# A decoder block on one Trainium2 core: where the token sums of the second half of the tokens are made

## The chip, the cores and the metric

The kernel runs as one program on one core of a Trainium2 chip. The core has five engines that matter here: TensorE (PE in the profile, with its weight loads as PEld), VectorE (DVE), ScalarE (ACT), GpSimd (POOL) and SyncE (SP), which in this kernel only issues DMA transfers. Each engine works through its own instructions in order. ACT also issues transfers, in order with its other work. The metric is the device time of one execution in microseconds (us); lower is better.

## The reference, cut to what matters

The block works on x of 2048 tokens with 1024 channels, in float32:

```python
h = _rmsnorm(x, norm_pre_mix)
proj = h @ w_in                                  # 1024 -> 5376
# three dilated attention groups, a chunked gMLP branch, merged by two sigmoid gates
y = merged @ w_out
x = x + _rmsnorm(y, norm_post_mix)

h = _rmsnorm(x, norm_pre_mlp)
a = relu(h @ w_mlp_in)                           # 1024 -> 4096
y = (a * a) @ w_mlp_out                          # 4096 -> 1024
x = x + _rmsnorm(y, norm_post_mlp)
```

What the change touches lies between `x = x + _rmsnorm(y, norm_post_mix)` and the first product of the MLP: how the transposed h gets from the one to the other.

## The kernel before

**The parts.** Part 1 (up to about 1120 us of the span) makes the projections, the attention and the gMLP branch. Part 2 merges the branches, multiplies by w_out, adds to x, normalizes, and transposes h. It goes by chunks of 512 tokens in the order 2, 3, 0, 1 (`chunks`, line 977), and in each chunk by four blocks of 128 tokens (`out_block`, line 900). Then comes the MLP: its first stage (h times w_mlp_in, relu and square), about 1449 to 2095 us, and its second stage (times w_mlp_out) up to the end.

**Every product is made of three.** A float32 operand is split into a rounded high part and the rest (`split`, line 67: ACT copies the high part, DVE subtracts it from the raw values), and a product is hi*hi + hi*lo + lo*hi, three matmuls. So an operand is ready for TensorE only when ACT and then DVE have split it.

**The first stage** uses a scheme with seven block products in place of eight. The tokens are worked in two halves of 1024, first tokens 1024 to 2047 (`first_half` = 1, chunks 2 and 3), then 0 to 1023 (`second_half` = 0, chunks 0 and 1). The right operands of a half are B11, B21 and B22, which are quarters of the transposed h, and T1 to T4, sums and differences of such quarters: the token sums. B11 and B21 are read from `h2_d`, a DRAM tensor of the transposed h; T1 to T4 and B22 from `t_d`, a DRAM tensor of the token sums. The left operands come from w_mlp_in, 256 columns at a time, numbered q = 0 to 15: A11 and A12 are plain quarters, S1 to S4 are sums that POOL makes of the raw weights with four instructions (`add_a`, lines 1064 to 1067), and A22 is plain. Product i of q, written (q, i), takes the pair `TERMS[i]`: 1 is A11 with B11, 2 is A12 with B21, 3 is S4 with B22, 4 is A22 with T4, 5, 6 and 7 are S1 to S3 with T1 to T3. Each is twelve matmuls (line 1093). (q, 2) adds to the bank of (q, 1), whose content ACT first copies to `xs` (line 1107).

**How the token sums are made before.** The second chunk of each half (`second = c % 2`, chunks 3 and 1) has, per block: two loads of the other chunk's transposed h from `h2_d` (line 924, on SP), the block's own transposes on TensorE (line 945) and two copies of them by ACT (line 946), four subtractions on POOL (lines 950 to 953), and the stores of five results to `t_d` (line 959; one transfer in chunk 3, three in chunk 1, where the tile is made of three places, tags `yt0` to `yt5`, line 1184). The first chunk of each half (2 and 0) stores its copies to `h2_d` instead (line 948). A block's second part (transposes, copies, sums) is put off and called by `flush`, its stores by `store`.

**The seam.** When chunk 1's last matmuls are issued, two blocks still wait to be flushed, and TensorE goes on with products of the first stage. From there to product (0, 3) the order on all engines is the order of the code (`as_written`, lines 1238 to 1297); low parts are held back until the product before them has been issued (`behind_product`, `rest`). SP's transfers in this stretch are: T2, raw weights for (3,1) and (2,2), the weights of q = 0, T3, raw weights for (4,1) and (3,2) in one tile, the stores of the flushed blocks, T1, the weights of q = 1, the raw weights for (4,2), the last block's stores, T4, B22, the weights of q = 2. A raw weight loaded alone goes to tag `ar`, which has two places, and is called by its q and n (n = 0 for A11, 1 for A12), so the raw weights for product (4, 2) are `raw_lone(h, 4, 1)`. From product (0, 3) on the order on ACT, DVE, POOL and SP is again that of a planner, which sends each engine the first instruction in code order that its own costs say is ready; TensorE's order is always that of the code.

**The rest of the first stage.** `order` lists the products; the loop at line 1334 asks for weights 14 products ahead and for their sums and splits 6 ahead. `ends` holds the last use of each right operand in the first half; behind it, `load_b` or `load_t` loads that of the second half into the same place.

Of the kernel before, what the change touches and what calls it, by code (L numbers as in the profile page):

```python
# [8 lines left out]
F32 = mybir.dt.float32  # L9
F32R = mybir.dt.float32r  # L10
# [31 lines left out]
def block_kernel(ctx, tc, a, out):  # L42
# [857 lines left out]
    def out_block(c, i, mg, mid):  # L900

        t0 = c * 512 + i * P
        isl = slice(i * P, (i + 1) * P)
        xt = bot.tile([P, D], F32, name=f"xr_{c}{i}", tag="xr")
        sp.dma_start(xt, x[t0:t0 + P, :])
        ss = sm.tile([P, 2], F32, name=f"ss_{c}{i}", tag="ss2")
        pp = [psum_mm(f"o_{c}{i}{n}") for n in range(2)]

        ks = [(n, k) for n in range(2) for k in range(KT)]
        if i == 0:  # L910
            ks.remove((0, KT - 1))
            ks.insert(KT + 2, (0, KT - 1))
        for m, (n, k) in enumerate(ks):
            if m == KT:
                mid()
            nsl = slice(n * 512, (n + 1) * 512)
            m = mg[k // 4]
            mm3(pp[n], m[:, 0, k % 4, isl], m[:, 1, k % 4, isl], wo[k][:, 0, nsl], wo[k][:, 1, nsl], k == 0, k == KT - 1)
        second = c % 2

        tt = tt_tile(c, i)
        if second:
            for o in range(2):
                sp.dma_start(tt[3 * o], h2_d[:, o * 4:o * 4 + 4, t0 - 512:t0 - 512 + P])
        y1 = bot.tile([P, D], F32, name=f"y1_{c}{i}", tag="y1", bufs=2)
        for n, p in enumerate(pp):
            nsl = slice(n * 512, (n + 1) * 512)
            junk = psum_aux(f"junk_{c}{i}{n}")
            act.activation(junk, p, AF.Square, accum_out=ss[:, n:n + 1])
            dve.tensor_mul(y1[:, nsl], p, gpost[:, nsl])  # L930
        s1 = sm.tile([P, 1], F32, name=f"s1_{c}{i}", tag="s1")
        dve.tensor_add(s1, ss[:, 0:1], ss[:, 1:2])
        r = rstd_of(sm, s1, 1, 1.0 / D, f"post{c}{i}")
        dve.scalar_tensor_tensor(xt, y1, r, xt, op0=OP.mult, op1=OP.add)
        s2 = sm.tile([P, 1], F32, name=f"s2_{c}{i}", tag="s2")
        act.activation(y1, xt, AF.Square, accum_out=s2)
        act.dma_start(x1_d[t0:t0 + P, :], xt)
        r2 = rstd_of(sm, s2, 1, 1.0 / D, f"pm{c}{i}")
        dve.scalar_tensor_tensor(y1, xt, r2, gmlp, op0=OP.mult, op1=OP.mult)
        yield  # L940
        for k in range(0, KT, 4):
            pt = psum_aux(f"pt_{c}{i}{k}")
            ht = tt[4 if k else 2] if second else tt[k // 4]
            for kk in range(4):
                pe.transpose(pt[:, kk * P:(kk + 1) * P], y1[:, (k + kk) * P:(k + kk + 1) * P], ident)
            act.activation(ht, pt.rearrange("p (k t) -> p k t", k=4), AF.Copy)
            if not second:
                act.dma_start(h2_d[:, k:k + 4, t0:t0 + P], ht)
        if second:
            pool.tensor_sub(tt[0], tt[2], tt[0])  # L950
            pool.tensor_sub(tt[1], tt[4], tt[0])
            pool.tensor_sub(tt[2], tt[4], tt[2])
            pool.tensor_sub(tt[3], tt[3], tt[1])
        yield
        if second:
            eng = act if store_eng is None else store_eng
            dst = t_d[c // 2].rearrange("p o k t -> p (o k) t")[:, :, i * P:(i + 1) * P]
            for o, t in tt["whole"]:
                eng.dma_start(dst[:, o * 4:o * 4 + t.shape[1]], t)
        yield  # L960
# [31 lines left out]

    def load_b(half, name):

        w = r3.tile([P, 2, 4, 512], F32R, name=f"{name}_{half}", tag=name, bufs=1)
        for k in range(0, 4, 2):
            t0, k0 = half * HALF, k + (4 if name == "B21" else 0)
            split_in(w[:, :, k:k + 2], h2_d[:, k0:k0 + 2, t0:t0 + 512], None, "act")
        b_[half, name] = w

# [25 lines left out]
    def raw_lones(half, *which):  # L1026

        w = wp3.tile([P, 2, 4, P], F32, name=f"w1r_lone{half}{which[0][0]}", tag="w1r", bufs=5)
        for m, (q, n) in enumerate(which):
            raw_lone(half, q, n, w[:, m])  # L1030
# [150 lines left out]
    def tt_tile(c, i):  # L1181

        if c == 1:
            w = [bot.tile([P, D], F32, name=f"tt{c}{i}{n}", tag=f"yt{i % 2 * 3 + n}").rearrange("p (k t) -> p k t", t=P)
                 for n in range(3)]
            whole = [(0, w[0]), (2, w[1]), (4, w[2][:, :4])]
            parts = {o: w[o // 2][:, o % 2 * 4:o % 2 * 4 + 4] for o in range(5)}
        else:
            w = ttp.tile([P, 5, 4, P], F32, name=f"tt{c}{i}", tag="tt")
            whole = [(0, w.rearrange("p o k t -> p (o k) t"))]  # L1190
            parts = {o: w[:, o] for o in range(5)}
        parts["whole"] = whole
        return parts
# [5 lines left out]
    for n, c in enumerate(chunks):  # L1199
        if n:  # L1200
            mg = merge(c, yt, {0: flush, 2: flush, 3: store, 6: store})
        for i in range(4):
            store()
            b = out_block(c, i, mg, flush_older)
            next(b)
            last.append(b)
            if n < 3 and not i:
                yt = load_y(chunks[n + 1])
                for dt in range(2):
                    for wch in range(2):  # L1210
                        load_gate(chunks[n + 1], dt, wch)
            if n == 3 and i == 1:
                e2r.close()
                rx = stack(e3, "rx", 1, side="right")
                r3 = stack(er, "r3", 1, side="right")
                for name in ("B11", "B21"):
                    load_b(1, name)
                for o, (q, n_) in enumerate(FIRST):
                    raw = gtp.tile([P, 512], F32, name=f"ar{n_}_{q}", tag=f"gt{o % 2}", bufs=3 - o % 2)
                    lone_a(1, q, n_, raw.rearrange("p (k c) -> p k c", k=4))  # L1220
# [17 lines left out]
    with as_written():  # L1238
        behind_product, store_eng = [], sp
        raw_t(h, "T2", tt_["T2"])  # L1240
        raw_lone(h, 3, 0)
        raw_lone(h, 2, 1)
        load_a(h, 0)
        raw_t(h, "T3", tt_["T3"])
        raw_lones(h, (4, 0), (3, 1))
        begin(0, 1)
        begin(1, 1)

        flush()
        store()  # L1250
        raw_t(h, "T1", tt_["T1"])
        split_t(h, "T2", (0,))
        begin(0, 2)
        load_a(h, 1)
        add_a(h, 0)
        split_t(h, "T2", (2,))
        split_lone(h, 3, 0)
        begin(2, 1)
        split_lone(h, 2, 1)
        begin(1, 2)  # L1260
        split_lone(h, 4, 0)
        begin(3, 1)
        raw_lone(h, 4, 1)

        flush()
        split_a(h, 0, "S2")
        split_lone(h, 3, 1)
        split_a(h, 0, "S1")
        begin(2, 2)
        store()  # L1270
        raw_t(h, "T4", tt_["T4"])
        raw_t(h, "B22", tt_["B22"])
        split_t(h, "T3")
        split_lone(h, 4, 1)
        begin(4, 1)
        split_a(h, 0, "S3")
        add_a(h, 1)
        begin(0, 6)
        split_t(h, "T1")
        begin(3, 2)  # L1280
        split_a(h, 0, "A22")
        begin(4, 2)
        split_a(h, 0, "S4")
        split_a(h, 1, "S2")
        split_t(h, "T4", (0,))
        begin(0, 7)
        split_t(h, "T4", (2,))
        split_a(h, 1, "S1")
        load_a(h, 2)
        begin(0, 5)  # L1290
        split_a(h, 1, "S3")
        split_t(h, "B22", (0,))
        begin(1, 6)
        split_t(h, "B22", (2,))
        begin(0, 4)
        behind_product, store_eng = None, None
        begin(0, 3)
# [31 lines left out]
    def raw_need(half, q, i):  # L1329
        if (half, q) not in araw and not (i < 3 and alone(q)):  # L1330
            load_a(half, q)

    n_last = order.index((second_half, NQ - TRAIL, 6))
    for n, z in enumerate(order[:n_last]):
        for z2 in order[n:n + 14]:
            raw_need(*z2)
        for z2 in order[n:n + 6]:
            if z2[:2] != (second_half, NQ - 2) or z2[2] < 3:
                need(*z2)
            elif z2[:2] not in sums_:  # L1340
                add_a(*z2[:2])
        product(*z)
        for name, last_use in ends.items():
            if z == last_use:
                (load_b if name in ("B11", "B21") else load_t)(second_half, name)
    er.close()
    middle.close()

# [426 lines left out]
```

## Time and profile before

| | us |
|---|---|
| median of three runs | 2731.72 (2729.7 to 2736.3) |
| the profiled execution's own time | 2733.0 |
| span of its profile, first to last instruction | 2731.3 |

| stretch of the span | us |
|---|---|
| parts 1 and 2, up to the first product of the MLP | 0 to 1448.7 |
| the seam, up to product (0, 3) | 1448.7 to 1505.9 |
| the MLP's first stage behind it | 1505.9 to 2095 |
| the MLP's second stage | 2095 to 2731.3 |

The time of an execution is some us longer than its span. In the profile a row of the timeline gives the start, the length, the engine, the line, the operation, what is written and read (out<-in, buffer numbers left out), and in brackets how long the engine was idle before and what released it. SPq and ACTq are the queues that issue transfers; the length in such a row is that of the issue, or of several issues merged in one row, and not that of the transfer. The windows give the busy time of each engine in a stretch, the clock granted to TensorE as a share of full speed, and how busy the 16 DMA engines were.

### The profile page before, as it was taken

To read this page: it belongs to the slowest core of one execution; us is meant where nothing else is said; L and a number is where in the kernel's file an instruction comes from. 1 tells how busy PE (TensorE), PEld (TensorE's weight loads), DVE (VectorE), ACT (ScalarE), POOL (GpSimd) and SP (SyncE) were. 2 spreads that over 40 slices of the span, in tenths; PEclk is the share of its full clock that TensorE was granted. 3 is DMA by queue.
4 is the path that set the end of the run, shared out by engine and by line. 5 is a ranking of instruction groups with operands and counts; after the bars stand their busy time and mean duration, and the time that the engine had idled before them with its cause. 6 is when DMAs were issued, how large, how long until landed. Compare 5 with 4: busy or idle time off the path is not lost. (4 is left out here: it accounts for less than half of the span.)

```text
span 2731.3 us, 34716 instructions
## 1 busy us (share of the span) xinstructions
PE 2688.8 (98%) x12674; PEld 2230.0 (82%) x12674; DVE 1583.9 (58%) x2677; ACT 1054.8 (39%) x2149; POOL 929.5 (34%) x750
## 2 busy tenths in 40 slices
PE   9999999999999999999998999999999999999998
PEld 8888888888888888787787788788887888888886
DVE  5655553344444345756567644655437887888866
ACT  5213111144444422444445545555544333333334
POOL 0351352200050023102005423223314766676645
PEclk9999999999999999999999999999999999999999
DMA  7445446366677755745559434654343222222236
GB/s 269 165 146 174 153 144 214 102 200 197 184 246 203 197 173 175 234 150 176 161 172 302 131 116 121 198 157 126 105 144 107 77 63 85 86 85 86 91 104 213
DMA packets 329725, 425.47 MB, mean 156 GB/s; under 512 B 52050, under 2 KB 205906, under 8 KB 329555
## 3 DMA queue, kind: packets, MB, share of 16 engines
q1 hardware_dynamic: 238016, 370.22, 43.2%
q10 hardware_dynamic: 91538, 53.03, 6.5%
q8 instruction: 100, 1.64, 0.3%
q14 instruction: 71, 0.57, 0.1%
HBM read 282.47 MB, written 140.71 MB: 155 GB/s over the span
## 5 line engine op out<-in xcount | busy, mean ns | idle before, releaser
L1627 PE MATMUL ya<-T_spots,s 128*128 128x512 f32 x1176 | 292.4, 392 | 3.4 <-ACT T_spots L70 3.4
L1627 PEld LDWEIGHTS ya<-T_spots,s 128*128 128x128 f32 x1176 | 221.5, 188 | 52.5 <-ACT T_spots L70 3.8
L70 ACT ACTIVATE s<-sraw 128x768 fp32r<-128x768 f32 (+1 forms) x184 | 127.4, 696 | 339.0 <-POOL sraw L1424 150.8
L1093 PE MATMUL aa<-B,A 128*128 128x512 f32 x768 | 186.8, 395 | 6.0 <-ACT xs L1107 5.2
L78 DVE TENSOR_TENSOR s<-sraw,s 128x512 fp32r<-128x512 f32 x171 | 179.5, 1074 | 6.8 <-ACT s L70 6.8
L1093 PEld LDWEIGHTS aa<-B,A 128*128 128x128 f32 x768 | 145.3, 190 | 40.0 <-ACT xs L1107 5.7
L1064 POOL TENSOR_TENSOR s<-w1r 128x512 f32<-128x512 f32 x32 | 42.3, 1322 | 395.1 <-DVE S L78 326.5
L1627 PE MATMUL yc<-T_spots,s 128*128 128x512 f32 x624 | 160.8, 391 | 0.0
L72 POOL TENSOR_SCALAR w_g<-w_g_r 128x1024 fp32r<-128x1024 f32 x32 | 34.1, 1082 | 344.8 <-PE g L97 316.1
L95 PE MATMUL x<-hT_a,wq 128*128 128x512 f32 x384 | 149.7, 390 | 0.0
L97 PE MATMUL x<-hT_a,wq 128*128 128x512 f32 x384 | 149.4, 389 | 0.0
L96 PE MATMUL x<-hT_a,wq 128*128 128x512 f32 x384 | 149.4, 389 | 0.0
L709 DVE TENSOR_REDUCE o<-po 128x256 f32<-128x512 f32 x48 | 33.1, 690 | 185.5 <-PE po L708 185.5
L1627 PEld LDWEIGHTS yc<-T_spots,s 128*128 128x128 f32 x624 | 117.2, 188 | 25.7
L70 ACT ACTIVATE hl<-r 128x512 fp32r<-128x512 f32 x48 | 30.4, 633 | 238.1 <-POOL r L307 89.0
L78 POOL TENSOR_TENSOR T_spots<-w2r,T_spots 128x512 fp32r<-128x512 f32 x70 | 104.5, 1520 | 7.5 <-ACT T_spots L70 7.5
L95 PE MATMUL g<-hT_b,w_g 128*128 128x512 f32 x256 | 104.8, 409 | 0.0
L95 PE MATMUL g<-hT_a,w_g 128*128 128x512 f32 x256 | 104.3, 407 | 0.0
L95 PE MATMUL o<-wo,mg 128*128 128x512 f32 x256 | 100.7, 393 | 2.8 <-ACT mg L70 1.6
L70 ACT ACTIVATE S<-w1r 128x512 fp32r<-128x512 f32 x96 | 60.0, 629 | 110.2 <-PE ac L1093 64.8
L1423 POOL TENSOR_TENSOR sraw<-sraw 128x256 f32<-128x256 f32 x56 | 41.4, 740 | 178.3 <-DVE s L78 163.9
L97 PE MATMUL o<-wo,mg 128*128 128x512 f32 x256 | 100.0, 391 | 0.5 <-DVE mg L78 0.4
(388 smaller groups left out, 7192.2 us busy)
## 6 DMA issues: line engine op xcount, KB each, us to landing
w1r<-in_w_mlp_in_dram SPq DMA_DIRECT2D x64, 512.0 KB, 3.6
sraw<-sd SPq DMA_DIRECT2D x128, 256.0 KB, 3.5
qk<-hl SPq DMA_DIRECT2D x24, 1024.0 KB, 5.6
qq<-qk SPq DMA_DIRECT2D x96, 256.0 KB, 5.0
w_g_r<-in_w_in_dram SPq DMA_DIRECT2D x32, 512.0 KB, 5.0
gated<-gt SPq DMA_DIRECT2D x64, 256.0 KB, 3.4
sd<-u ACTq DMA_DIRECT2D x64, 256.0 KB, 3.6
w2r<-in_w_mlp_out_dram SPq DMA_DIRECT2D x16, 1024.0 KB, 7.9
```

The costliest lines, as they stand in the source:

```text
L70: act.activation(hi, src, AF.Copy)
L72: pool.tensor_scalar(hi, src, 1.0, 1.0, op0=OP.mult, op1=OP.mult)
L78: (pool if lo_eng == "pool" else dve).tensor_sub(lo, src, f32(hi))
L95: pe.matmul(ps, lh, rh, start=start, stop=False)
L96: pe.matmul(ps, lh, rl, start=False, stop=False)
L97: pe.matmul(ps, ll, rh, start=False, stop=stop)
L709: dve.tensor_reduce(ot[:, :, j * 64:(j + 1) * 64], po.rearrange("p (b h e) -> p b e h", b=4, h=2), axis=AX.X, op=OP.add)
L1064: pool.tensor_add(s1, a21, a22)
L1093: pe.matmul(p, w[:, l, k, :], h[:, r, k, :], start=i in (1, 6, 5) and not k and not n, stop=k == 3 and n == 2, skip_group_check=True)
L1423: pool.tensor_add(a22, a21, a22)
L1627: pe.matmul(p, s[:, l], w[r], start=i in (1, 2, 5) and not m and not o, stop=m == 1 and o == 2, skip_group_check=True)
```

## The change

It has four parts. First, only chunk 3 still makes token sums in its blocks. Chunk 1 stores its transposed h to `h2_d`, as chunk 0 does (on SP where `store_eng` is set). Its tiles are one place each (`yt0` to `yt3`). Second, a new function `sums_t(k)`, called four times behind products (5, 4) to (8, 4) of the first half, loads quarters of the stored h of both chunks, makes the four sums with four subtractions on POOL, and stores them to `t_d`. Third, B22 of the second half is loaded from `h2_d` by `load_b`. Fourth, at the seam, the raw weights for (4, 2) go to a place of their own (`spare`, one of the six places of tag `xs`) and are asked for early, and T4 and B22 are asked for where those weights were, ahead of the last flush.

```diff
-        second = c % 2
+        second = c == 3
...
             if not second:
-                act.dma_start(h2_d[:, k:k + 4, t0:t0 + P], ht)
+                (act if store_eng is None else store_eng).dma_start(h2_d[:, k:k + 4, t0:t0 + P], ht)
...
     def load_b(half, name):
 
-        w = r3.tile([P, 2, 4, 512], F32R, name=f"{name}_{half}", tag=name, bufs=1)
+        w = (bp if name == "B22" else r3).tile([P, 2, 4, 512], F32R, name=f"{name}_{half}", tag=name, bufs=1)
         for k in range(0, 4, 2):
-            t0, k0 = half * HALF, k + (4 if name == "B21" else 0)
+            t0, k0 = half * HALF + (512 if name == "B22" else 0), k + (0 if name == "B11" else 4)
...
         if c == 1:
-            w = [bot.tile([P, D], F32, name=f"tt{c}{i}{n}", tag=f"yt{i % 2 * 3 + n}").rearrange("p (k t) -> p k t", t=P)
-                 for n in range(3)]
-            whole = [(0, w[0]), (2, w[1]), (4, w[2][:, :4])]
-            parts = {o: w[o // 2][:, o % 2 * 4:o % 2 * 4 + 4] for o in range(5)}
+            w = bot.tile([P, D], F32, name=f"tt{c}{i}", tag=f"yt{i}").rearrange("p (k t) -> p k t", t=P)
+            whole = []
+            parts = {o: w[:, o * 4:o * 4 + 4] for o in range(2)}
...
                 rx = stack(e3, "rx", 1, side="right")
+                spare = rx.tile([P, 512], F32, name="ar1_4", tag="xs", bufs=LEAD + 1)
...
         raw_lones(h, (4, 0), (3, 1))
+        raw_lone(h, 4, 1, spare.rearrange("p (k c) -> p k c", k=4))
         begin(0, 1)
...
         begin(3, 1)
-        raw_lone(h, 4, 1)
+        raw_t(h, "T4", tt_["T4"])
+        raw_t(h, "B22", tt_["B22"])
 
         flush()
...
         store()
-        raw_t(h, "T4", tt_["T4"])
-        raw_t(h, "B22", tt_["B22"])
         split_t(h, "T3")
...
+    eq = ExitStack()
+    tq = stack(eq, "tq", 1)
+
+    def sums_t(k):
+
+        w = tq.tile([P, 2, 512], F32, name=f"tq{k}", tag="tq", bufs=1)
+        b11, b12 = w[:, 0], w[:, 1]
+        b21, b22 = (wp3.tile([P, 512], F32, name=f"tq{k}{n}", tag="ar", bufs=2) for n in range(2))
+        t0 = second_half * HALF
+        for t, kk, c in ((b11, k, 0), (b12, k, 1), (b22, k + 4, 1), (b21, k + 4, 0)):
+            sp.dma_start(t, h2_d[:, kk, t0 + c * 512:t0 + c * 512 + 512])
+        pool.tensor_sub(b11, b12, b11)
+        pool.tensor_sub(b12, b22, b12)
+        pool.tensor_sub(b22, b22, b11)
+        pool.tensor_sub(b21, b21, b22)
+        for name, t in (("T1", b11), ("T3", b12), ("T2", b22), ("T4", b21)):
+            sp.dma_start(t_d[second_half][:, T_AT.index(name), k], t)
...
         product(*z)
+        if z[0] == first_half and z[2] == 4 and z[1] in range(5, 9):
+            sums_t(z[1] - 5)
+            if z[1] == 8:
+                eq.close()
         for name, last_use in ends.items():
             if z == last_use:
-                (load_b if name in ("B11", "B21") else load_t)(second_half, name)
+                (load_b if name[0] == "B" else load_t)(second_half, name)
```

## The prediction

> **What bounds the kernel now.** I read the page first, then TensorE's waits, then its order of time where the code touched by the diff runs, and last the queues of the engines that it waits for there.
>
> ```profile
> PE 2688.8 (98%) x12674; PEld 2230.0 (82%) x12674; DVE 1583.9 (58%) x2677; ACT 1054.8 (39%) x2149; POOL 929.5 (34%) x750
> ```
>
> TensorE is the bound, and the diff adds and removes no matmul. So the change can only win or lose what TensorE spends waiting, plus what a wait does to its clock. Two of TensorE's longer waits, at chunk 3's end (L945) and at the start of the second MLP stage (L1627), lie where the diff touches nothing. Those from 1300 to 1560 us are (us in total, times, longest):
>
> ```profile
> PE aa L1093 <- ACT xs L1107: 5.2, 1, 5.2
> PE ac L1093 <- DVE B_first L85: 1.6, 2, 1.0
> PE o L95 <- ACT mg L70: 1.2, 1, 1.2
> PE aa L1093 <- DVE A L85: 0.7, 1, 0.7
> ```
>
> The third is chunk 0's. The others lie at the seam from chunk 1 into the MLP's first stage. In chunk 1 itself TensorE waits for nothing, so what goes there is worth nothing by itself. At the seam the order of time on TensorE is (start, length, instructions, wait before):
>
> ```profile
> 1454.94 8.87 PE L1093 MATMUL aa<-B,A 128*128 128x512 f32 x38
> 1464.54 2.59 PE L1093 MATMUL aa<-B,A 128*128 128x512 f32 x10 [0.72 <-DVE A L85]
> 1466.96 1.03 PE L945 MATMUL pt<-ident,y 128*128 128x128 f32 x8
> ...
> 1473.30 3.21 PE L1093 MATMUL ab<-T_first,S 128*128 128x512 f32 x12
> 1476.35 2.93 PE L1093 MATMUL aa<-B,A 128*128 128x512 f32 x12
> 1484.53 5.52 PE L1093 MATMUL aa<-B,A 128*128 128x512 f32 x12 [5.25 <-ACT xs L1107]
> 1489.88 2.94 PE L1093 MATMUL ab<-T_first,S 128*128 128x512 f32 x12
> ...
> 1501.03 0.39 PE L1093 MATMUL ac<-B_first,S 128*128 128x512 f32 x1
> ...
> 1505.94 2.96 PE L1093 MATMUL ab<-T_first,S 128*128 128x512 f32 x12
> 1508.73 2.95 PE L1093 MATMUL ac<-T_first,S 128*128 128x512 f32 x12
> ```
>
> An undisturbed group of twelve takes 1508.73 - 1505.94 = 2.79 us, so one matmul 0.232. The losses at the seam are then:
> - products (3,2) and (4,2), from 1476.35 to 1489.88: 13.53 us for two groups, 13.53 - 5.58 = **7.95 lost**. Only 5.25 of it is the wait; the twelve matmuls behind it take 5.35 instead of 2.79.
> - (0,2) to (3,1), 1454.94 to 1466.96: 12.02 us for 48 matmuls, 48 x 0.232 = 11.14, **0.88 lost**.
> - (0,6), 1473.30 to 1476.35: 3.05, **0.26 lost**.
> - (0,3), 1501.03 to 1505.94: 4.91, **2.12 lost**.
>
> Why the matmuls behind the wait are slow, and how loaded the seam is, the windows say (busy of PE, PEld, DVE, ACT, POOL, granted clock, DMA share, GB/s):
>
> ```profile
> 1484.50:1489.40 4.90, 4.80 (x10) 3.31 (x11) 4.90 (x4) 4.14 (x6) 3.95 (x3) 0.50 1.08 328
> 1448.70:1503.80 55.10, 48.02 (x204) 37.63 (x202) 41.23 (x43) 32.33 (x52) 33.66 (x22) 0.94 0.96 324
> 1503.80:1553.00 49.20, 48.63 (x210) 39.22 (x209) 32.38 (x41) 25.09 (x43) 25.09 (x17) 1.00 0.43 134
> ```
>
> After the long idle time the clock stands at 0.50 for about five us. And through the whole seam the DMA engines are full (0.96), while just behind it they are not (0.43). So a transfer asked for late arrives late. Who made ACT late, by the queues of ACT and SP:
>
> ```profile
> 1470.46 1.33 ACT L946 ACTIVATE tt<-pt 128x512 f32<-128x512 f32 x2 [2.70 <-POOL w1r L1067]
> 1483.36 0.63 ACT L70 ACTIVATE A<-ar 128x512 fp32r<-128x512 f32 x1 [5.54 <-DMA ar<-in_w_mlp_in_dram]
> ```
> ```profile
> 1457.61 0.97 SPq L1023 DMA_DIRECT2D w1r_lone<-in_w_mlp_in_dram  x2
> 1460.06 6.57 SPq L959 DMA_DIRECT2D td<-tt  x3
> ...
> 1475.46 0.68 SPq L1023 DMA_DIRECT2D ar<-in_w_mlp_in_dram  x1
> ```
>
> The raw weights for product (4,2) are asked for at 1475.46, behind the stores of token sums, and have landed when ACT goes on at 1483.36. ACT, in order, stands 5.54 us before the split of them; behind it stands the copy L1107 that empties the bank which product (4,2) adds to.
>
> **The change part by part.**
>
> *Spare place for the raw weights of (4,2).* The load moves to the slot behind the two w1r_lone loads, 1460.06 at the latest, since the old queue issues its next DMA there. Landing, from the two loads just before it:
>
> ```profile
> DMA to landing us min/median/max: 7.9/8.1/8.2
> ```
>
> 1460.06 + 8.2 = 1468.3, 15 us earlier. What is late next is ACT's own queue. TensorE, 0.88 ahead, ends (3,1) at 1466.1; then ACT does the copy of xs (0.6), two of tt (1.1, to 1468.0), three splits of 0.6 (1469.7), two steps on c after (2,2) ends (1.3) and a DMA issue (0.6; 1471.6), two splits of T3 (2.0), the split for (4,2) (0.6) and L1107 (0.6): 1474.8. TensorE gets to (4,2) at 1489.88 - 5.35 - 1.14 - 5.25 = 1478.1. Margin 3.3 us: the wait goes, and with it the slow clock, **-7.95**.
>
> *Sums out of chunk 1.* Gone from each of the four row blocks: two loads (L924), four subtractions on POOL, three stores; in their place two stores of 256 KB. ACT's 2.70 before tt goes too: that tile waited for the place that block 1's stores still held (the row names POOL, which had long ended), and now has a place of its own. POOL's sums of weights for q = 0 stand behind token sums, and POOL's work slows DVE:
>
> ```profile
> 1463.89 1.73 POOL L1064 TENSOR_TENSOR s<-w1r 128x512 f32<-128x512 f32 x1
> ```
> ```profile
> 1462.71 3.47 DVE L85 TENSOR_TENSOR A<-ar,A 128x512 fp32r<-128x512 f32 x2
> 1490.75 0.68 DVE L85 TENSOR_TENSOR A<-w1r,A 128x512 fp32r<-128x512 f32 x1
> 1500.08 2.31 DVE L85 TENSOR_TENSOR B_first<-B_first 128x1024 fp32r<-128x1024 f32 x1
> ```
>
> The same DVE subtraction (128x512) takes 0.68 alone and 1.74 beside POOL. The two at 1462.71 are the operand that (3,1) waits for: without POOL's block-2 sums the first is done by 1463.4 and **-0.88** follows; S2 of (0,6), whose sums start at 1463.89 behind the token sums, can start when its weights have landed: **-0.26**. After that DVE's margins are the thin ones: by the same walk its half of the split for (4,2) is done at 1477.0 against 1478.5, and T1's at 1482 against 1485.
>
> *(0,3) stays.* Its two waits come from DVE reaching B_first at 1500.08, and then running beside POOL's sums of weights for q = 2. Both are tied to TensorE's own progress (the bank of (0,4) is read between the two B_first halves), not to the landing of B22. **0**; bounds -2.12 (both go) and +1.
>
> *T4 and B22 ahead of the second flush.* Four loads come earlier; the last two stores of chunk 1 come later, behind them. They hold yt3, which S4 of q = 0 takes. By the queue's throughput (324 GB/s; about 10 MB ahead of them from 1449) they land at 1480 to 1482, and ACT wants the place at 1482.6. **0**; at most +4, two slow landings.
>
> *New work in the first stage (four times).* Per k: four loads of 256 KB, four POOL subtractions, four stores; the trace has no such rows. Nearest (KB, us to landing):
>
> ```profile
> tt<-h2d SPq DMA_DIRECT2D x16, 256.0 KB, 3.7
> td<-tt SPq DMA_DIRECT2D x3, 256.0 KB, 6.3
> ```
>
> Loads 3.7 to 8.2, subtractions 4 x 1.30 to 1.73 (both lengths in the POOL rows here), stores 3.7 to 6.3: 12.6 to 21.4 us each, 50 to 86 for all. The planner sends what it can at once: these two weights are loaded 167 us ahead of their split.
>
> ```profile
> 1495.78 0.81 SPq L1023 DMA_DIRECT2D ar<-in_w_mlp_in_dram  x2
> 1662.40 0.63 ACT L70 ACTIVATE A<-ar 128x512 fp32r<-128x512 f32 x1
> ```
>
> So I expect the sums to run from about 1490 on, not at their line, in POOL's gaps (25.09 busy of 49.20 above). Cover is wide there: the T operands are wanted only in the second half of the tokens, over 200 us later, and DMA stands at 0.43. SP's stores now wait for POOL, and behind them on SP stand the loads of later weights, which are asked for 14 products ahead (14 x 2.79 = 39 us), longer than a whole set takes. If it failed, the cost is that of the slower rival below. I take **0**, bounds 0 to +8, the DVE time that 16 subtractions of POOL could hold there (16 x 0.5, from 0.68 above to 1.20 in rival 4's row).
>
> [...]
>
> Loads of B22 from h2_d, the other order of places and the moved lone loads at the stage's end cost nothing: they have over 20 us.
>
> **Sum**: -7.95 - 0.88 - 0.26 = -9.1 on the profiled execution's 2733.0 (span 2731.3), so 2723.9. The median of before is 2731.7, 1.3 below that execution: 2722.6.
>
> **The rivals.**
> 1. *(0,3) clears too* (POOL's sums of q = 2 come later than B_first, because token sums stand before them): -11.2, **2720.5**. Against it: the DVE add between the halves.
> 2. *A shorter wait takes the old one's place at the seam*: the late stores that hold yt3, or the thin DVE margins. For it: DMA at 0.96. Price up to 4: -5.1, **2726.6**.
> 3. *POOL in order, slower.* Token sums that wait for their loads stand in front of POOL's sums of weights. The lead there, by the rows of q = 8 in the settled stage:
>
> ```profile
> 1599.46 1.30 POOL L1064 TENSOR_TENSOR s<-w1r 128x512 f32<-128x512 f32 x1 [13.71 <-DVE S L78]
> 1602.22 1.62 POOL L1066 TENSOR_TENSOR w1r<-s,w1r 128x512 f32<-128x512 f32 x1
> 1614.45 2.94 PE L1093 MATMUL ab<-T_first,S 128*128 128x512 f32 x12
> ```
>
> From 1603.84 to 1614.45 are 10.6 us, less two for the splits. Four subtractions (5.2 to 6.9) plus a wait for landing (3.7 to 8.2) are 8.9 to 15.1, so it decides once a set holds POOL beyond 8.6 us out of turn; it then costs up to 6.5 a set, and past a wait like (4,2)'s the half clock for 2.6 more. At 4.5, the middle of 0 and 9.1, and four sets: +18 - 9.1 = +9, **2740.6**. Against it: the 13.71 us of idle time before each set.
> 4. *DVE held by POOL in the first stage*:
>
> ```profile
> 1601.48 1.20 DVE L78 TENSOR_TENSOR S<-w1r,S 128x512 fp32r<-128x512 f32 x1
> ```
>
> If all 8 us come through, -1, **2730.6**. Against it: DVE is busy 32 of 49 us there.
> 5. *It doesn't do what it says*: the planner leaves ACT as late by another load: **2731.7**.
>
> **How the numbers follow.** A measurement of this kernel tells 0.3%, 8.2 us, from no change; the forecast lies just beyond it. Chances: forecast 0.47 (0.43 of it beyond 8.2), rival 1 0.10, rival 2 0.22, rival 3 0.10, rival 4 0.08 (0.02 of it slower), rival 5 0.03. Faster 0.43 + 0.10 = 0.53; slower 0.10 + 0.02 = 0.12; same 0.35. The range goes from just below rival 1, 2719, to 2731, which takes in rivals 2 and 4 and leaves rival 3, half of the rest and what no case foresees: two in ten.
>
> **What would show it.** In the profile after: no wait on L1107 and a granted clock of 1.00 from (4,2) on; the load for (4,2) right behind the w1r_lone loads; ACT's tt copies without a wait; the two waits on B_first still there; token sums on POOL between 1485 and 1570, and no TensorE wait from there to 1700. The prediction is wrong if TensorE waits on ACT S or DVE S in 1480 to 1570, or if (4,2) still waits over 3 us.

## The result, and the profile after

The changed kernel takes 2742.83 us (median of five executions, 2740.25 to 2743.71) against 2732.17 for the kernel before, measured beside it (five, 2729.7 to 2736.3). The ratio is 1.0034, with a 95% interval of 1.0022 to 1.0046: it is slower by about 0.3%, where 0.3% faster was forecast. The profiled execution has a span of 2741.5 us, 10.2 longer than before.

TensorE's busy time on the page, and then the waits of TensorE that answer to those shown of before (total, times, longest):

```profile
PE 2695.7 (98%) x12674; PEld 2232.7 (81%) x12674; DVE 1572.8 (57%) x2677; ACT 1056.6 (39%) x2149; POOL 922.8 (34%) x750
```
```profile
PE ab L1093 <- DVE u L1118: 7.0, 4, 3.1
...
PE ac L1093 <- ACT B_first L70: 4.2, 1, 4.2
...
PE aa L1093 <- ACT A L70: 3.0, 1, 3.0
...
PE ac L1093 <- DVE B_first L85: 1.5, 1, 1.5
```

The long wait on L1107 is gone, as forecast. Three others have come, and the order of time on TensorE says where:

```profile
1464.73 5.98 PE L1093 MATMUL aa<-B,A 128*128 128x512 f32 x12 [3.04 <-ACT A L70]
...
1502.08 0.79 PE L1093 MATMUL ac<-B_first,S 128*128 128x512 f32 x1 [4.23 <-ACT B_first L70]
1504.40 4.63 PE L1093 MATMUL ac<-B_first,S 128*128 128x512 f32 x11 [1.52 <-DVE B_first L85]
...
1536.44 5.49 PE L1093 MATMUL ab<-T_first,A 128*128 128x512 f32 x12 [3.09 <-DVE u L1118]
```

Each of the three is followed by matmuls at half clock (windows of the same kernel; the clock stands behind POOL's column):

```profile
1464.70:1470.50 5.80, 5.65 (x12) 3.86 (x13) 2.61 (x4) 2.73 (x5) 0.00 (x0) 0.50 1.04 411
1502.00:1508.80 6.80, 5.20 (x12) 3.77 (x13) 4.57 (x4) 2.24 (x4) 6.57 (x4) 0.53 0.95 297
1536.40:1542.00 5.60, 5.56 (x13) 4.41 (x14) 3.56 (x5) 1.89 (x3) 0.53 (x2) 0.50 0.58 144
```

By the starts of single matmuls against 0.232 us each, the losses are **A**, 6.1 us at product (3,1); **B**, 8.4 at (0,3); **C**, 6.1 at 1536; and 3.2 in small ones between them. Together they are 23.8, where the same stretch of before lost 11.1 (8.0, 2.1 and 1.0). That is 12.7 more; the first stage starts 1.7 earlier than in the execution of before, and the rest of the span differs by under 1: 10.2 in all.

**Where A comes from.** ACT around it:

```profile
1456.91 0.63 ACT L1103 ACTIVATE c<-c 128x512 f32<-128x512 f32 x1
1462.51 0.54 ACTq L1099 DMA_DIRECT2D sd<-c  x1
1463.10 1.06 ACT L70 ACTIVATE T_first<-T_first 128x1024 fp32r<-128x1024 f32 x1 [5.55 <-DMA w1r_lone<-in_w_mlp_in_dram]
1464.06 0.61 ACT L70 ACTIVATE A<-ar 128x512 fp32r<-128x512 f32 x1
```

c is ready at 1457.54, but ACT issues the store of it only at 1462.51, 4.97 us later, and everything behind that issue waits too, the split for (3,1) among it. What ended the idle time, says the row, is a load of w1r_lone, which has nothing to do with c. The two loads of it were issued on SP's queue at 1451.64 and 1453.09; for that tile and stretch the profile says when they landed:

```profile
L1023 SPq DMA_DIRECT2D w1r_lone<-in_w_mlp_in_dram x2: 333/333/333, 1451.6 to 1453.1; - x2
...
DMA to landing us min/median/max: 9.3/9.8/10.2
```

1453.09 + 9.3 = 1462.4, and 0.1 later ACT's store goes. The trace gives the reason. Each issue of SP and ACT in it names the signal (a semaphore) that tells its landing, and the 1194 of them use eight such signals between them, numbers 100, 102 and 105 to 110. No transfer is issued before the one that had its signal last has landed, in all 1038 cases of this trace for which the landing before is known, and in all 1020 of before's; the nearest issue begins 0.02 us behind that landing. ACT's store had drawn the signal of the second w1r_lone load (105), which landed at 1462.44.

**Where B comes from.** The same thing a second time, on ACT:

```profile
1495.10 0.63 ACT L1103 ACTIVATE u<-u 128x512 f32<-128x512 f32 x1
1499.89 0.52 ACTq L1099 DMA_DIRECT2D sd<-u  x1
1500.45 0.63 ACT L70 ACTIVATE S<-w1r 128x512 fp32r<-128x512 f32 x1 [4.72 <-DMA w1r<-in_w_mlp_in_dram]
1500.99 1.99 ACT L70 ACTIVATE B_first<-B_first 128x1024 fp32r<-128x1024 f32 x2
```

The w1r load that had the store's signal (102) was issued at 1492.63 and landed at 1499.81; the store goes at 1499.89. SP's queue shows what it stood behind (and, in its first row, that the load into the spare place went early, as the change meant), and POOL's order what comes of it:

```profile
1454.64 0.33 SPq L1023 DMA_DIRECT2D ar<-in_w_mlp_in_dram  x1
1455.90 0.33 SPq L1343 DMA_DIRECT2D tq<-h2d  x1
...
1483.82 6.50 SPq L1349 DMA_DIRECT2D td<-tq  x4
1490.43 2.15 SPq L1343 DMA_DIRECT2D tq<-h2d  x4
1492.63 0.42 SPq L1052 DMA_DIRECT2D w1r<-in_w_mlp_in_dram  x1
...
1514.91 1.90 SPq L1343 DMA_DIRECT2D tq<-h2d  x4
1520.11 0.32 SPq L1349 DMA_DIRECT2D td<-tq  x1
1520.53 1.83 SPq L1052 DMA_DIRECT2D w1r<-in_w_mlp_in_dram  x4
```
```profile
1518.78 1.30 POOL L1344 TENSOR_TENSOR tq<-tq 128x512 f32<-128x512 f32 x1 [4.33 <-DMA tq<-h2d]
...
1524.40 1.29 POOL L1064 TENSOR_TENSOR s<-w1r 128x512 f32<-128x512 f32 x1 [0.21 <-DMA w1r<-in_w_mlp_in_dram]
```

The first load of a token-sum set goes in the middle of the seam, and POOL has made all four sets by 1524.2. Their stores on SP wait for POOL, the loads of the next set wait behind them, and behind those stand the weights.

**Where C comes from.** The weights for the next columns are asked for at 1520.53 there; POOL can begin their sums at 1524.40, and ACT's split of the first of them waited 9.02 us:

```profile
1525.73 0.63 ACT L70 ACTIVATE S<-s 128x512 fp32r<-128x512 f32 x1 [9.02 <-POOL s L1064]
```

Behind that split the subtractions on DVE come late too, and DVE stands in them when TensorE needs the sum u that empties the bank for its next product. That is the wait of 3.09 us at 1536.44:

```profile
1534.04 1.75 DVE L78 TENSOR_TENSOR A<-w1r,A 128x512 fp32r<-128x512 f32 x1
1535.71 0.67 DVE L1118 TENSOR_TENSOR u<-xs,ab 128x512 f32<-128x512 f32 x1
```

In the kernel before, the issue of those weights and POOL's first sum of them come ten us earlier (SP's queue, then POOL), and TensorE loses nothing there:

```profile
1510.29 18.51 SPq L1052 DMA_DIRECT2D w1r<-in_w_mlp_in_dram  x6
```
```profile
1514.13 1.29 POOL L1064 TENSOR_TENSOR s<-w1r 128x512 f32<-128x512 f32 x1 [8.36 <-DMA w1r<-in_w_mlp_in_dram]
```

### The profile page after: what moved, and what is told of

Same layout as the page of the kernel before. It is cut to its first block, busy times and chain, and to the rows that moved or that the text cites. A ratio compares the mean times of both kernels' runs of the same rounds, so it can differ in the third digit from the quotient of the medians.

```text
span 2741.5 us, 34740 instructions
## 1 busy us (share of the span) xinstructions
PE 2695.7 (98%) x12674; PEld 2232.7 (81%) x12674; DVE 1572.8 (57%) x2677; ACT 1056.6 (39%) x2149; POOL 922.8 (34%) x750
## 5 line engine op out<-in xcount | busy, mean ns | idle before, releaser
L95 PE MATMUL g<-hT_b,w_g 128*128 128x512 f32 x256 | 104.8, 409 | 0.0
L95 PE MATMUL o<-wo,mg 128*128 128x512 f32 x256 | 100.6, 393 | 1.0 <-ACT mg L70 0.9
L97 PE MATMUL g<-hT_b,w_g 128*128 128x512 f32 x256 | 100.4, 392 | 0.0
```

The source lines that it names most:

```text
L95: pe.matmul(ps, lh, rh, start=start, stop=False)
L97: pe.matmul(ps, ll, rh, start=False, stop=stop)
```

## The experiments

Three theories were to be told apart. **S**: a store of ACT's is held until an SP load lands whose signal it has drawn, and ACT's splits stand behind it (A). **P**: the token sums run too early, and their transfers on SP and their sums on POOL stand ahead of the weights (B and C). **D**: the seam's loads are simply late, because the DMA engines are full (0.96 of them busy in before's seam), whoever issues what.

**1. The spare place alone** (with the earlier T4 and B22 that belong to it; token sums as before):

```diff
+                spare = rx.tile([P, 512], F32, name="ar1_4", tag="xs", bufs=LEAD + 1)
...
+        raw_lone(h, 4, 1, spare.rearrange("p (k c) -> p k c", k=4))
...
-        raw_lone(h, 4, 1)
+        raw_t(h, "T4", tt_["T4"])
+        raw_t(h, "B22", tt_["B22"])
...
-        raw_t(h, "T4", tt_["T4"])
-        raw_t(h, "B22", tt_["B22"])
```

> The kernel before with the spare place for the raw weights of (4,2) and the earlier T4 and B22, the token sums of chunk 1 left where they were. Theory S (landing slots: an issue waits until an earlier transfer that had its slot has landed, the slots are dealt in the planner's order over SP and ACT, so ACT's own stores of s come to wait for SP's loads): SP is as late here as before, so ACT's first store gets an early slot; the 5.25 us wait on L1107 and its slow clock go, about 8 us are won: 2722 to 2727. Theory P (only the token sums in the first stage cost time): the same, 2723. Theory D (the DMA engines are full and whatever is asked for lands late): the wait moves to another load, 2729 to 2733.

Measured: 2733.99 against 2733.11, ratio 1.0003 (0.9993 to 1.0012). The wait on L1107 ahead of (4,2) is gone here too, and a loss of 7.5 us, nearly as large as the 8.0 that went, stands at (3,1). TensorE, then ACT:

```profile
1470.54 0.73 PE L1093 MATMUL aa<-B,A 128*128 128x512 f32 x2 [3.31 <-ACT A L70]
```
```profile
1468.32 0.54 ACTq L1099 DMA_DIRECT2D sd<-c  x1
1468.91 1.06 ACT L70 ACTIVATE T_first<-T_first 128x1024 fp32r<-128x1024 f32 x1 [5.82 <-DMA w1r_lone<-in_w_mlp_in_dram]
```

The store of c, ready at 1463.08, was held 5.24. So the edit meant for the wait moves the wait, and gains nothing. Judged by the time alone, D's forecast is the nearest and those of S and P fail; S had expected an early signal for this store, and it had that of a w1r_lone load.

**2. The token sums alone**, without the spare place and the earlier T4 and B22 (the other three parts of the diff).

> The changed kernel without the spare place and with T4 and B22 asked for where they were before. Theory S: SP runs ahead without the stores of sums, ACT's stores get late slots, a wait at (3,1) or near it and the early sums' waits after the seam stay: 2738 to 2746. Theory P: the waits after the seam stay (about 16 us lost), the seam itself loses what it lost before: 2741. Theory D: less traffic in the seam, 2730 to 2735.

Measured: 2736.08 against 2733.11, ratio 1.0010 (1.0000 to 1.0019). No store of ACT's is held over 1 us, and (3,1) loses 0.9: A belongs to the spare place. There is no wait on L1107 ahead of (4,2) either, without the spare place. B (6.7) and C (5.0) stay, so they belong to the sums. The time lies between the forecasts of the three theories and meets none.

B comes another way here, since no store is held. TensorE, then DVE:

```profile
1497.57 5.06 PE L1093 MATMUL ac<-B_first,S 128*128 128x512 f32 x11 [3.86 <-DVE B_first L85]
```
```profile
1489.57 2.35 DVE L85 TENSOR_TENSOR T_first<-T_first 128x1024 fp32r<-128x1024 f32 x1
```

That subtraction takes 1.22 in the kernel before, and the split of S behind it 1.79 here against 0.69. Both run here beside POOL's token sums (1489.54 to 1494.76), and in before while POOL is idle (1488.61 to 1498.31). With the two splits of S ahead of them (2.40 here, 1.29 in before) that is 3.3 us more, and DVE gets to B_first late. So the early sums can bring B in two ways: by a held store, as in the changed kernel, or by a DVE that takes longer beside POOL, as here.

**3. The whole change, the sums held to their line**: the planner may issue nothing of a set before the last instruction that SP and POOL were given ahead of it.

```diff
-            sums_t(z[1] - 5)
+            with ExitStack() as es:
+                for e in (mybir.EngineType.SP, mybir.EngineType.Pool):
+                    es.enter_context(tc.issue_after(next(i for i in reversed(nc.cur_bb.bb.instructions) if i.engine == e)))
+                sums_t(z[1] - 5)
```

> The changed kernel with each of the four sets of token sums queued behind the last load and the last POOL instruction traced before it, so that the planner can't send them ahead to the seam. Theory S: the wait at (3,1), 6 us with the slow clock, stays, since ACT's first store still has the slot of a w1r_lone load; those at (0,3) and (1,4) go but for about 2 us: 2727 to 2731. Theory P: the seam is clean too, 2722 to 2724. Theory D: 2724 to 2728.

Measured: 2728.64 against 2733.11, ratio 0.9981 (0.9972 to 0.9990), 14.2 below the change. The sums begin at 1571, 1591, 1610 and 1629, between POOL's sums of weights (the first row of them below), at no cost that TensorE shows; B is back at the 2.1 that before has, C is gone, and 3.5 are left at (3,1), where the store of c was held 4.31. P stands for B and C; its forecast of a clean seam fails. S's forecast comes true: A is a cost of its own.

```profile
1571.56 1.56 POOL L1344 TENSOR_TENSOR tq<-tq 128x512 f32<-128x512 f32 x1 [8.26 <-DMA tq<-h2d]
```

**4. The whole change, the seam's stores of c and u issued by SP:**

```diff
-            act.dma_start(s_d[q, half][:, :, o, :], t.rearrange("p (i c) -> p i c", i=4))
+            (act if store_eng is None else store_eng).dma_start(s_d[q, half][:, :, o, :], t.rearrange("p (i c) -> p i c", i=4))
```

> The changed kernel with the stores of s in the seam issued by SP in place of ACT; the sums stay early. Theory S: ACT waits for no slot in the seam, so the wait at (3,1) goes and that at (0,3) shrinks to about 2 us; the one at (1,4), where POOL's sums of weights come late, stays: 2730 to 2736. Theory P: all waits stay, 2741 to 2744. Theory D: they stay too, under other names, 2740 or more.

Measured: 2739.34, ratio 1.0022 (1.0012 to 1.0032). A is gone: TensorE runs the 48 matmuls of (0,2) to (3,1) in one piece. B is 1.9, but C has grown to 7.4 and 5.7 in two places, so that the time misses S's range as well. The early sums are still there; that SP now has more to wait for is the likely reason, and not shown.

```profile
1452.18 11.15 PE L1093 MATMUL aa<-B,A 128*128 128x512 f32 x48
...
1507.11 4.63 PE L1093 MATMUL ab<-T_first,S 128*128 128x512 f32 x10 [2.33 <-DVE S L78]
```

**5. Both: sums held, seam's stores on SP** (the edits of 3 and 4).

> The whole change, with the four sets of token sums held back to their own line and the seam's stores of c and u issued by SP instead of ACT. Theory (ACT's own store, and all behind it on ACT, waits for the landing of an SP load): the 3.5 us that the kernel with the sums held still loses at product (3,1), 1465.7 to 1467.4, go, and nothing else comes: about 2728.6 - 3.5 = 2725. Rival (the wait only changes its queue: SP now waits for c and u, and the loads behind it come late): losses on ACT S, DVE S or DVE u of 2 to 6 us between 1475 and 1535, 2728 to 2734. Rival (the seam's loads are late by throughput alone): (3,1) loses its 3.5 us as before, on ACT A or DVE A, 2728.6.

Measured: 2725.49 against 2733.59, ratio 0.9967 (0.9955 to 0.9980). No loss at (3,1), 2.3 at (0,3), nothing else up to 1700: as S expects, and against D, since the same loads are asked for.

**6. The spare place and the seam's stores on SP**, token sums as before (the edits of 1 and 4).

> The spare place and the earlier T4 and B22 alone, token sums as before, the seam's stores of c and u issued by SP. Theory: without ACT's held store (5.24 us at 1468.32 with the spare place alone) the 7.5 us at (3,1) go and the wait on L1107 stays away: 2734.0 - 7.5 = 2726.5. Rival (in the full seam the loads themselves are late, whoever issues the store): a wait of 3 us or more and its half clock stay at (3,1), (3,2) or (4,2), 2731 to 2736.

Measured: 2736.25, ratio 1.0012 (1.0003 to 1.0021). S failed here: the wait on L1107 is back, and 11.8 are lost from 1481 to 1497. TensorE, then ACT:

```profile
1487.77 1.22 PE L1093 MATMUL aa<-B,A 128*128 128x512 f32 x2 [6.05 <-ACT xs L1107]
```
```profile
1483.56 0.60 ACT L1102 ACTIVATE c<-aa 128x512 f32<-128x512 f32 x1 [7.79 <-DMA sd<-c]
```

Now ACT stands before it writes c, since an earlier c still holds the place; its store was issued by SP at 1476.72, behind six stores and two loads of chunk 1's token sums. With those in SP's queue, neither ACT (experiment 1) nor SP is a good place to issue these stores. (0,3) loses the 2.1 that before loses.

**7. Sums held, without the spare place and the earlier T4 and B22** (the edit of 3 on the kernel of 2).

> The sums taken out of chunk 1 and held back to their own line, without the spare place and without the earlier T4 and B22. If the wait on L1107 goes because chunk 1's stores no longer stand ahead of the load for (4,2) (it was gone with the sums alone, without the spare place), then the spare place is worth nothing by itself: no wait over 1 us at (4,2), about 0.9 lost at (3,1), 2733.1 - 8.0 = 2725. If the spare place is what removes it: 5 us of waiting and the half clock at (4,2), 2732 to 2733.

Measured: 2725.43 against 2733.59, ratio 0.9970 (0.9960 to 0.9980). No wait on L1107 ahead of (4,2), 0.7 lost at (3,1), 2.1 at (0,3). With chunk 1's token sums out of SP's queue the load for (4,2) goes in its old place early enough: at 1465.39 (before 1475.46), and ACT's split follows at 1472.96 (before 1483.36). SP's queue, and ACT:

```profile
1465.39 0.84 SPq L1023 DMA_DIRECT2D ar<-in_w_mlp_in_dram  x1
```
```profile
1472.96 0.63 ACT L70 ACTIVATE A<-ar 128x512 fp32r<-128x512 f32 x1
```

So the change doesn't need the spare place to remove the wait. The sums' leaving chunk 1 does it alone.

**8. The whole change, the sixteen stores of the sums issued by POOL:**

```diff
-            sp.dma_start(t_d[second_half][:, T_AT.index(name), k], t)
+            pool.dma_start(t_d[second_half][:, T_AT.index(name), k], t)
```

> The whole change, sums as early as the planner likes, their sixteen stores issued by POOL's queue instead of SP's. Theory (the stores that wait for POOL stand on SP ahead of the weight loads): the loss on DVE u at 1536 to 1543 (6.1) goes and the one at (0,3) (8.4) falls to 2 to 4; the 6.1 at (3,1) stays: 2742.8 - 6.1 - 5 = 2732. Rival (POOL's own order is what is late, its token sums waiting for their loads ahead of the sums of weights): both stay, 2740 to 2746 with POOL's issues on top.

Measured: 2750.66, ratio 1.0064 (1.0050 to 1.0078), beyond both expectations. C has not gone but grown, to 4.2 and 11.9. It isn't the stores on SP alone, then. The eight loads of two sets hold SP for 19 us by themselves, since by the code a set's places come free only when the set before has been stored, and the weights stand behind them:

```profile
1506.87 19.02 SPq L1343 DMA_DIRECT2D tq<-h2d  x8
1525.98 1.91 SPq L1052 DMA_DIRECT2D w1r<-in_w_mlp_in_dram  x4
```

How much of the rest is POOL's own order and its issues (0.56 each) this run doesn't part.

**9. As 3, but the load into the spare place written five products later**, behind product (2,1):

```diff
-        raw_lone(h, 4, 1, spare.rearrange("p (k c) -> p k c", k=4))
         begin(0, 1)
...
         begin(2, 1)
+        raw_lone(h, 4, 1, spare.rearrange("p (k c) -> p k c", k=4))
         split_lone(h, 2, 1)
```

> The whole change with the sums held to their line, and the load into the spare place written five products later, behind product (2,1). Theory (a store of ACT's waits for the landing of the transfer eight earlier in the written order, whatever that is): one transfer fewer stands ahead of ACT's first store of c, so it falls behind a load of T2 that landed at about 1452 instead of behind a w1r_lone load that lands at 1463: issue at 1458 with no hold over 1 us, the loss at (3,1) 3.5 to under 1, 2728.6 - 2.8 = 2725.8, with the spare place still in use. Rival (the spare place's own 256 KB make the full seam's loads late): nothing is taken out of the seam, so the hold and the 3.5 us stay: 2728.6.

Measured: 2725.23 against 2732.34, ratio 0.9974 (0.9964 to 0.9984). The store of c goes 0.03 after c is ready; (3,1) loses 1.4.

**10 and 11. As 3, with only one of the two seam edits each**: the spare place without the earlier T4 and B22, and the earlier T4 and B22 without the spare place.

> The sums held, the spare place as in the change, T4 and B22 loaded where they were before. Theory: the store of c still falls behind the w1r_lone load (the spare place's load is what shifts it): held 4 to 5 us, 3 to 4 lost at (3,1), 2728 to 2729. Rival (T4 and B22 ahead of the second flush are what fills the seam and makes ACT's store late): under 1 lost, 2725.5.

> The sums held, T4 and B22 loaded early as in the change, no spare place (the load for (4,2) where it was before). Theory: as without either part, no held store, under 1 lost at (3,1), no wait on L1107: 2725.5. Rival (the early loads of T4 and B22 cost): the hold and 3 to 4 us at (3,1), or a new wait at (4,2), 2728 to 2729.

Measured: 2728.81 (0.9984, 0.9976 to 0.9993) and 2723.32 (0.9968, 0.9956 to 0.9981), both against 2732.34. The first has the hold and 5.1 lost at (3,1), the second 1.2 and no hold. ACT of the one and of the other, the same two instructions:

```profile
1461.90 0.54 ACTq L1099 DMA_DIRECT2D sd<-c  x1
1462.48 1.06 ACT L70 ACTIVATE T_first<-T_first 128x1024 fp32r<-128x1024 f32 x1 [5.03 <-DMA w1r_lone<-in_w_mlp_in_dram]
```
```profile
1457.95 0.54 ACTq L1099 DMA_DIRECT2D sd<-c  x1
1458.54 1.06 ACT L70 ACTIVATE T_first<-T_first 128x1024 fp32r<-128x1024 f32 x1 [0.62 <-ACT c L1103]
```

For the first store of c, the trace's landing signals give this table (us):

| kernel | c ready | the signal's transfer before | landed | store issued | lost at (3,1) |
|---|---|---|---|---|---|
| before | 1459.22 | a load of T_first | 1456.20 | 1459.25 | 1.0 |
| after | 1457.54 | w1r_lone | 1462.44 | 1462.51 | 6.1 |
| 1, spare place alone | 1463.08 | w1r_lone | 1468.25 | 1468.32 | 7.5 |
| 3, sums held | 1459.21 | w1r_lone | 1463.44 | 1463.52 | 3.5 |
| 10, 3 without early T4, B22 | 1457.45 | w1r_lone | 1461.82 | 1461.90 | 5.1 |
| 7, 3 without both | 1457.88 | a load of T_first | 1451.80 | 1457.91 | 0.7 |
| 9, 3 with the spare load later | 1462.15 | a load of T_first | 1456.31 | 1462.18 | 1.4 |
| 11, 3 without the spare place | 1457.92 | a load of T_first | 1451.81 | 1457.95 | 1.2 |

In every row the store goes within 0.1 us of the later of the two events. The spare place's load, written ahead of the store, shifts which signal the store draws; written behind it, it doesn't. The w1r_lone loads take as long to land in number 9 (9.8 to 10.1 us) as in number 3 (10.0), and little less in numbers 7 (9.4 to 9.7) and 11 (9.0 to 9.3), and hold nothing in those three, so D falls as the cause of the hold; how long a hold lasts is still set by how late such a load lands (the four holds, 4.31 to 5.24 us, end 0.07 or 0.08 behind it). The ratios of 3 and 9 lie within each other's intervals; it is the 3.5 and 1.4 lost at (3,1), and the store's row, that tell them apart. The version with the lowest median is number 11: the change without its spare place and with the sums held, 0.3% faster than before (the ratios of numbers 5, 7 and 9 lie within its interval, that of 3 at its edge).

## Why the prediction was wrong, step by step

**"New work in the first stage ... I take 0": this step failed.** It foresaw that the planner would run the sums from about 1490 on, and saw POOL's gaps and the DMA engines' 0.43 as wide cover. But the queue that counts was SP's. The argument that weights are asked for "14 products ahead (14 x 2.79 = 39 us), longer than a whole set takes" took a distance in the code for one in time: in before, those weights are issued at 1510.29 and POOL begins on them at 1514.13, after 8.36 us of waiting for them. The lead is 3.8 us there, not 39, and ten us later, as in the changed kernel, TensorE waits 3.09 at C. The early sums cost 2742.83 - 2728.64 = 14.2 us (experiment 3), against the 0 taken and the bound of 8. By the traces of the two kernels, B, C and the small losses fall from 17.7 to 2.1. The bound was worked out from DVE's sharing with POOL alone; that is what made B in experiment 2, but in the changed kernel the weights and the store of u came late first. This is rival 3 at 0.10, on the side of the loads on SP; its price came out near (2740.6) because it was a middle of bounds, and it knew nothing of A.

**"Margin 3.3 us: the wait goes ... -7.95": right in what it says of L1107, wrong in what follows, and credited to the wrong part.** The load was issued at 1454.64, earlier than the 1460.06 counted on, and the wait went. But the walk through ACT's queue set the issue of a store down at 0.6 us, its length in a row; the hold before it was 5.0 us in the changed kernel and moved the wait to (3,1), half clock and all. Rival 2 had a shorter wait in the old one's place, priced up to 4. The spare place alone was worth nothing (experiment 1: 7.5 lost for 8.0 gained), and the 8 us come from the sums leaving chunk 1 (experiment 7, where the seam loses 0.7 + 2.1 against 11.1).

**"-0.88" at (3,1) and "-0.26" at (0,6).** The first was not there: 0.7 to 1.4 are lost at (3,1) even in kernels without a held store, against 1.0. It goes only with the stores on SP (experiment 5). The second came: (0,6) runs undisturbed in experiment 7. Of the -1.14 one had 0.26.

**"(0,3) stays": right by itself.** It loses 2.1 to 2.3 in every kernel with the sums held. The 8.4 of the changed kernel come from the step that failed. **T4 and B22 at 0: right**: 10 against 3, and 11 against 7, lie within each other's intervals.

**The sum.** Of the 12.7 that the changed kernel loses more, B gives 6.3, C 6.1, the small ones 3.2 and A 5.1, less the 8.0 at (4,2) that went. Without the early sums and the held store the number of the prediction came out near: it gave -9.1, and experiments 7, 9 and 11 gave 7 to 9 below the kernel measured beside them. Nearly all of that is the -7.95, which came by another part of the change than the one it was credited to; in that the near number is luck.

## What to carry to other kernels

When a planner or a framework deals a few landing signals to transfers of several queues, as the eight here, the price of an issue can be far more than its length in the row (0.54 us in the changed kernel, behind a hold of 4.97): it includes the wait for the landing of whatever had the signal before. Look at who ended the idle time of the instruction behind it, and at the compute that stands behind an engine's own stores. Work with "wide cover" still needs its place in every queue that it uses; the lead that counts is that from issue to first use in the trace, not the distance in the code. And when a wait goes, try each part of the edit alone: here the part that was meant to remove it only moved it.

## What the runs showed of the hardware

The half clock doesn't follow from the length of the idle time alone, as two waits of these traces show. At the end of the first stage TensorE waits for the same operand, 2.35 us before and 2.34 after. TensorE and the window behind it, of before and then of after:

```profile
2084.15 3.03 PE L1093 MATMUL ab<-T,A 128*128 128x512 f32 x12 [2.35 <-DVE u L1118]
```
```profile
2083.90:2089.00 5.10, 4.85 (x21) 4.00 (x22) 4.64 (x8) 3.45 (x6) 2.54 (x4) 1.00 0.54 157
```
```profile
2094.36 4.50 PE L1093 MATMUL ab<-T,A 128*128 128x512 f32 x12 [2.34 <-DVE u L1118]
```
```profile
2094.00:2099.00 5.00, 4.64 (x13) 3.69 (x14) 3.08 (x6) 2.41 (x4) 2.43 (x4) 0.66 0.54 159
```

Before, twelve matmuls take 3.03 us at a clock of 1.00; after, 4.50 at 0.66 (0.50 from 2096.0 to 2097.5). So two equal waits for the same operand can be followed by different clocks; what decides between them the two traces don't show. A prediction of a wait's price has to carry both cases: here they are 1.5 us apart.
